# One-bank sums for the feed-forward outputs, one chain of 1/rms for two tiles, and masks made on GpSimd before the diff attention

## Chip, core and metric

The kernel runs on one core of one Trainium2 chip. The metric is the device time of one execution in microseconds (us). The core has a matrix engine (TensorE, PE in the profile), a vector engine (VectorE, DVE), a scalar engine (ScalarE, ACT), a general engine (GpSimd, POOL) and queues that issue transfers (SyncE, SP). Every engine runs its own instructions strictly in the order in which they stand, and waits where an instruction needs a result of another engine.

## What is computed

One sequence of 256 tokens, width 1024, float32. Two layers of a first block come first: each has a feed-forward, a mixer (nsa in layer 0, diff attention in layer 1), and a second feed-forward, all added to `x`. A second block follows (adaLN, moba attention with rope beside an rwkv recurrence) and ends with PEER, which reads far more weights than the rest.

```python
def rmsnorm(x, g):
    xf = x.astype(f32)
    y = xf * lax.rsqrt(jnp.mean(xf * xf, axis=-1, keepdims=True) + EPS)
    return (y * g.astype(f32)).astype(x.dtype)
def swiglu(x, w_in, w_out):
    a, b = jnp.split(x @ w_in, 2, axis=-1)
    return (jax.nn.silu(a) * b) @ w_out
# first_block, layer = 0 (nsa), 1 (diff)
        x = x + 0.5 * swiglu(rmsnorm(x, ffn1_norm[layer]), ffn1_w_in[layer], ffn1_w_out[layer])
        hn = rmsnorm(x, mix_norm[layer])
        x = x + y                         # y = nsa_mixer(hn, ...) or diff_mixer(hn, ...)
        x = x + 0.5 * swiglu(rmsnorm(x, ffn2_norm[layer]), ffn2_w_in[layer], ffn2_w_out[layer])
# diff attention
        p = masked_softmax(sc, dist >= 0)
        a = p[:, :, 0] - lmbda * p[:, :, 1]
        return jnp.einsum('bhts,bhsd->bhtd', a.astype(v.dtype), v)
# ... then o = rmsnorm(o, subln) * (1.0 - lam_init), and o @ w_out
# second_block
    qm = rope_partial(rms_norm(qm.reshape(...), q_norm_g[l]), positions)
    o_rwkv = rwkv7_time_mix(zr, zk, zv, zw, za, zg, ...)
```

## The kernel before

**Stages.** They follow one another: `ffn1_0` (to about 206 us), nsa (391), `ffn2_0` (591), `ffn1_1` (787), `diff` (925), `ffn2_1` (1112), the second block (1400), PEER. `x` lies in SBUF as two tiles of 128 tokens (tile 0 and tile 1).

**Matmuls.** Each is float32 in two parts: a weight tile `raw` is fetched by SP, ACT writes its rounded part `whi` (L124), DVE the rest `wlo` (L125, `raw` minus `whi`), and PE adds three products (L184 to L186) or two (L192, L193). There are four `raw` buffers and six for the split parts. The activations are split alike: PE transposes 128 columns of `x` (`bank<-ident,x`, L234), ACT writes the gained high part `xx` (L270), DVE the low part (L271).

**A feed-forward** keeps the hidden values transposed in `hT` and `lT`. `out_proj` sums the output for tile 0, then for tile 1, each in two halves of 512 columns. A half fills one 2 KiB bank of PSUM; both halves lie in one tile `pair` of two banks. For tile 1 the last weights are taken first for half 0 and then for half 1, so that half 0 is finished earlier; the line `x<-pair,x` (L375, DVE) adds a finished half to `x`. Waits are kept per tile: L375 on half 0 is a reader of the whole pair. The next stage begins with eight transposes of each tile of `x`; those of tile 0 are put ahead by `tc.high_priority(AHEAD_T)`. Beside `ffn2_0`, DVE also adds up `acc` for the second block's adaLN from weights `araw` (L943). The second block takes its transposes of `x` as products with a diagonal `rd` (L958 on DVE, L236 on PE).

**1/rms.** `rstd(i)` squares tile i on ACT (L210) and takes the inverse root of the sum by 14 small instructions (`ms`, `rsg`, `rst`, `rsy`, L214 and L168 to L178). They run on DVE, in the first feed-forward on POOL, one chain for each tile.

**The diff attention** works on four heads and one tile at a time. For each group the probabilities `pr` are subtracted (L861 to L864, DVE) and transposed, L871 multiplies them by `dv` into a bank, ACT squares the result (`dsq`), DVE finds its 1/rms (`dss`, then the same small instructions), and L878 writes the normalised `do`. `do` is transposed (L234), split into `doh` (ACT) and `dol` (DVE, L271), and used by the output matmuls (`bank<-whi,doh`).

**Constants of the second block.** `rope_tables` (sine and cosine of the positions) and `rwkv_consts` stand in the program behind `diff()`; their instructions are drawn into it where an engine's order has room. `rwkv_consts` makes `cmask` and six triangular masks: DVE fills `lm` (L1004), POOL cuts it with three selects (L985), DVE copies two corners of it to `lmask` (L1012). `lm` has two buffers. Nothing reads them before the rwkv stage near 1180 us.

Of the kernel before, what the change touches and what calls it, by code (L numbers as in the profile page):

```python
# [20 lines left out]
F32 = mybir.dt.float32  # L21
# [6 lines left out]
OP = mybir.AluOpType  # L28
# [57 lines left out]
class K:  # L86
# [115 lines left out]

    def rstd(self, i, eps=1e-6, parts=1, early=False):
# [175 lines left out]
    def ffn(self, gain, win, wout, first=False):  # L379
        nc, tc = self.nc, self.tc  # L380
        with ExitStack() as ctx:
# [4 lines left out]
            self.mm = ctx.enter_context(tc.tile_pool(name=self.name("pairs"), bufs=3, space=PSUM, reuse_waits="tile"))  # L386
# [5 lines left out]
            if first:  # L392
# [5 lines left out]
                with tc.manual_schedule(engines={mybir.EngineType.Activation, mybir.EngineType.DVE}):  # L398
# [18 lines left out]
                    rs = [self.rstd(i, early=RSP > 0) for i in range(2)]  # L417
# [27 lines left out]
            for f in range(2, 22):  # L445
# [66 lines left out]
    def head_rs(self, src, n, tag):  # L512
# [22 lines left out]
    def nsa(self):  # L535
        nc, tc, d = self.nc, self.tc, self.d
        with ExitStack() as ctx:
# [46 lines left out]
            for b in range(2):  # L584
                pm = self.proj_chunk("ni", (3 + b,))
                for i in range(2):
# [3 lines left out]
                    r = self.head_rs(kk, 4, "nk")  # L590
# [204 lines left out]
    def diff(self):  # L795
        nc, tc, d = self.nc, self.tc, self.d
        with ExitStack() as ctx:
# [29 lines left out]
            def project(c):  # L827
                pm = self.proj_chunk("di", (c,), by_tile=c == 2)
                for i in range(2):
# [5 lines left out]
                    r = self.head_rs(qk, 8, "dq")  # L835
# [145 lines left out]
    def rwkv_consts(self, pool):  # L981
# [5 lines left out]
        tc_pool = lambda n, b: self.tc.tile_pool(name=self.name(n), bufs=b, reuse_waits="tile")  # L987

        self.cmask = f("cmask", [P, 2, P])
        nc.vector.memset(self.cmask, 1.0)  # L990
        for j in range(2):
            sel(self.cmask[:, j], [[1, P]], j - 1, -1)
        nc.vector.memset(self.cmask[0:64, :, 64:], 0.0)
# [5 lines left out]
        with tc_pool("lm", 2) as tmp:  # L999
            for lv in range(6):  # L1000
                b = 1 << lv
                n = P // (2 * b)
                w = tmp.tile([P, P], F32, name=self.name("lm"), tag="lm")
                nc.vector.memset(w, -1.0)  # L1004
                m = w.rearrange("p (k a u) -> p k a u", a=2, u=b)

                sel(m, [[-2 * b, n], [0, 2], [0, b]], 0, 1)
                sel(m, [[2 * b, n], [0, 2], [0, b]], b - 1, -1)
                sel(m, [[0, n], [1, 2], [0, b]], -1, 0)
                for e in range(2):  # L1010
                    r = slice(64 * e, 64 * e + 64)
                    nc.vector.tensor_copy(self.lmask[r, lv], w[r, r])  # L1012
# [1025 lines left out]
```

## Time and profile before

| | |
|---|---|
| runs | 2220.10, 2226.38, 2228.98 us; median 2226.38 |
| profiled execution | 2228.67 us; span in the trace 2226.9 us |
| busy in the span | PE 98%, DVE 75%, ACT 52%, POOL 1% |
| mean granted clock of PE | 0.987 |

The profiled execution took 2.29 us longer than the median of the runs, and 1.8 us lie around its span. Times in a timeline are counted from the start of the span.

### The profile page before, as it was taken

Reading aid. Unit: us, or ns where it says so; the run is one execution under the profiler, and the core shown is the slowest. Engines: PE = TensorE matmul, PEld = TensorE weight load, DVE = VectorE, ACT = ScalarE, POOL = GpSimd, SP = SyncE. Lnnn points to the kernel's source line nnn. Section 1 sums busy time; section 2 is a strip of 40 time slices with the busy share of each in tenths; the row PEclk is TensorE's granted clock in tenths of the full one; section 3 lists DMA queues with packets and bytes.
Section 4 is the critical chain, followed back from the end, with each engine's and each line's share of the span. In section 5 each row is a group of like instructions: output and inputs, shape, how many; then the busy total and the mean of one; then the engine's idle time right before and its main releaser. Section 6 shows DMA issues by size and latency. Waiting matters only on the chain.

```text
span 2226.9 us, 34952 instructions
## 1 busy us (share of the span) xinstructions
PE 2173.3 (98%) x13218; PEld 1835.4 (82%) x13218; DVE 1677.5 (75%) x3367; ACT 1168.1 (52%) x1853; POOL 33.1 (1%) x75
## 2 busy tenths in 40 slices
PE   8999999999999999899999999999999999999999
PEld 7887646888788876688788777899999998888887
DVE  6866575998688488788487667798858888997555
ACT  6554475654455476455355534445544445555443
POOL 2000000000000000200000000000000000000000
PEclk9999998999999999999999999999999999999999
DMA  6555333877665543355442215545554445545554
GB/s 219 190 190 181 126 106 114 294 273 266 229 218 184 189 153 118 113 189 189 153 146 95 77 48 170 172 159 192 181 180 170 164 169 199 175 175 180 196 191 151
DMA packets 107561, 383.28 MB, mean 172 GB/s; under 512 B 13440, under 2 KB 13824, under 8 KB 107392
## 3 DMA queue, kind: packets, MB, share of 16 engines
q1 hardware_dynamic: 103392, 374.39, 48.7%
q10 hardware_dynamic: 3360, 4.55, 0.7%
q8 instruction: 104, 1.70, 0.3%
q0 software_dynamic: 640, 2.11, 0.3%
q14 instruction: 65, 0.53, 0.1%
HBM read 378.89 MB, written 2.11 MB: 171 GB/s over the span
## 4 chain that ended last, share of the span: by engine, by line
PE 85%; DVE 9%; ACT 2%; DMA 2%; issue 1%; POOL 1%; SPq 0%; ACTq 0%; DVEq 0%; POOLq 0%
PE pair L192 13%; PE pair L193 7%; PE pout L184 5%; PE pout L186 5%; PE pout L185 5%; PE pu L184 5%; PE pu L185 5%; PE pu L186 5%; PE pair L184 4%; PE bank L184 4%; PE pair L186 4%; PE pair L185 4%; PE bank L185 4%; PE bank L186 4%; DVE wlo L125 3%; PE pw L1704 1%
## 5 line engine op out<-in xcount | busy, mean ns | idle before, releaser
L124 ACT ACTIVATE whi<-raw 128x1024 fp32r<-128x1024 f32 x654 | 690.8, 1059 | 704.8 <-PE pout L185 136.5
L125 DVE TENSOR_TENSOR wlo<-raw,whi 128x1024 fp32r<-128x1024 f32 x654 | 797.5, 1222 | 292.6 <-ACT whi L124 283.1
L192 PE MATMUL pair<-xx,whi 128*128 128x512 f32 x1280 | 450.2, 396 | 0.0
L193 PE MATMUL pair<-xx,wlo 128*128 128x256 f32 x1280 | 359.1, 281 | 0.0
L184 PE MATMUL pu<-xx,whi 128*128 128x256 f32 x1024 | 292.6, 286 | 1.1 <-ACT H L1660 1.1
L185 PE MATMUL pu<-xx,wlo 128*128 128x256 f32 x1024 | 289.8, 283 | 0.0
L186 PE MATMUL pu<-xx,whi 128*128 128x256 f32 x1024 | 289.8, 283 | 0.0
L192 PEld LDWEIGHTS pair<-xx,whi 128*128 128x128 f32 x1280 | 240.8, 188 | 56.1 <-issue 0.2
L193 PEld LDWEIGHTS pair<-xx,wlo 128*128 128x128 f32 x1280 | 242.2, 189 | 0.5 <-issue 0.2
L184 PE MATMUL pout<-whi,hs 128*128 128x512 f32 x512 | 201.6, 395 | 1.2 <-ACT hs L1760 1.2
L186 PE MATMUL pout<-wlo,hs 128*128 128x512 f32 x512 | 199.4, 390 | 0.0
L185 PE MATMUL pout<-whi,hs 128*128 128x512 f32 x512 | 199.3, 389 | 0.0
L184 PEld LDWEIGHTS pu<-xx,whi 128*128 128x128 f32 x1024 | 196.4, 192 | 1.3 <-ACT H L1660 1.3
L185 PEld LDWEIGHTS pu<-xx,wlo 128*128 128x128 f32 x1024 | 196.5, 192 | 0.0
L186 PEld LDWEIGHTS pu<-xx,whi 128*128 128x128 f32 x1024 | 196.3, 192 | 0.0
L184 PE MATMUL pair<-whi,hT 128*128 128x512 f32 x352 | 138.9, 395 | 6.6 <-DVE x L375 6.6
L186 PE MATMUL pair<-wlo,hT 128*128 128x512 f32 x352 | 139.5, 396 | 0.0
L185 PE MATMUL pair<-whi,lT 128*128 128x512 f32 x352 | 138.6, 394 | 0.0
L184 PE MATMUL bank<-whi,xx 128*128 128x512 f32 x288 | 118.0, 410 | 0.6 <-DVE rsg L168 0.6
L185 PE MATMUL bank<-whi,xx 128*128 128x512 f32 x288 | 116.0, 403 | 0.0
L186 PE MATMUL bank<-wlo,xx 128*128 128x512 f32 x288 | 115.2, 402 | 0.0
L186 PEld LDWEIGHTS pout<-wlo,hs 128*128 128x128 f32 x512 | 96.1, 188 | 20.5
(564 smaller groups left out, 3509.8 us busy)
## 6 DMA issues: line engine op xcount, KB each, us to landing
raw<-in_pu_dram SPq DMA_DIRECT2D x128, 512.0 KB, 3.5
raw<-in_pv_dram SPq DMA_DIRECT2D x128, 512.0 KB, 3.5
raw<-in_f1i_dram SPq DMA_DIRECT2D x88, 512.0 KB, 3.6
raw<-in_f2i_dram SPq DMA_DIRECT2D x88, 512.0 KB, 4.3
araw<-in_wada_dram SPq DMA_DIRECT2D x48, 512.0 KB, 4.6
raw<-in_f1o_dram SPq DMA_DIRECT2D x44, 512.0 KB, 3.5
raw<-in_f2o_dram SPq DMA_DIRECT2D x44, 512.0 KB, 4.2
raw<-in_wi_dram SPq DMA_DIRECT2D x28, 512.0 KB, 3.4
```

The source lines that it names most:

```text
L124: nc.scalar.activation(hi, raw, AF.Copy)
L125: nc.vector.tensor_tensor(lo, raw, hi.bitcast(F32), op=OP.subtract)
L184: mm(out, lh, rh, start=start, stop=False)
L185: mm(out, ll, rh, start=False, stop=False)
L186: mm(out, lh, rl, start=False, stop=stop)
L192: mm(out, lh, rr, start=start, stop=False)
L193: mm(out[:, 0], ll, rr[:, 0], start=False, stop=stop)
L1704: nc.tensor.matmul(pw[:, t], b[:, t // Q, :, t % Q], a[:, t // Q, :, :, t % Q], start=True, stop=True)
```

## The change

1. `out_proj` of every feed-forward gets single banks: the pool of pairs is closed behind the hidden layer, and six one-bank tiles are opened. With `self.pairs` false, `pair()` hands out two banks with a name each.
2. The first feed-forward calls `rstds`: both squares write one tile of two columns, and one chain of 14 instructions on GpSimd works on both columns.
3. `rope_tables` and `rwkv_consts` are called ahead of `diff()`, and the fills, selects and copies of the masks are all GpSimd's; `lm` has one buffer.
4. Four tags of `head_rs` become one (`hr`), and the slice of its scratch tile is taken earlier. The instructions stay the same.

```diff
+    def rstds(self, early=False):
+        nc = self.nc
+        junk = self.sm.tile([P, D], BF16, name=self.name("junk"), tag="junk", bufs=1)
+        v = self.sm.tile([P, 2], F32, name=self.name("ms"), tag="ms")
+        for i in range(2):
+            nc.scalar.activation(junk, self.x[:, i], AF.Square, accum_out=v[:, i:i + 1])
+        e = nc.gpsimd if early else nc.vector
+        e.tensor_scalar(v, v, 1.0 / D, 1e-6, op0=OP.mult, op1=OP.add)
+        y = self.rsqrt(v, [P, 2], "rs", e=e)
+        return [y[:, i:i + 1] for i in range(2)]
...
-            self.mm = ctx.enter_context(tc.tile_pool(name=self.name("pairs"), bufs=3, space=PSUM, reuse_waits="tile"))
+            inner = ctx.enter_context(ExitStack())
+            self.mm = inner.enter_context(tc.tile_pool(name=self.name("pairs"), bufs=3, space=PSUM, reuse_waits="tile"))
...
-                    rs = [self.rstd(i, early=RSP > 0) for i in range(2)]
+                    rs = self.rstds(early=RSP > 0)
...
+            inner.close()
+            self.pairs = False
+            self.banks(ctx, mm=6)
             self.out_proj(hT, lT, wout, 22, self.add_x(0.5))
             self.extra = None
-            self.pairs = False
...
-        nc.vector.memset(self.cmask, 1.0)
+        nc.gpsimd.memset(self.cmask, 1.0)
...
-        with tc_pool("lm", 2) as tmp:
-            for lv in range(6):
...
-                nc.vector.memset(w, -1.0)
...
-                    nc.vector.tensor_copy(self.lmask[r, lv], w[r, r])
+        for lv in range(6):
+            b = 1 << lv
+            n = P // (2 * b)
+            w = pool.tile([P, P], F32, name=self.name("lm"), tag="lm")
+            nc.gpsimd.memset(w, -1.0)
+            m = w.rearrange("p (k a u) -> p k a u", a=2, u=b)
+            sel(m, [[-2 * b, n], [0, 2], [0, b]], 0, 1)
+            sel(m, [[2 * b, n], [0, 2], [0, b]], b - 1, -1)
+            sel(m, [[0, n], [1, 2], [0, b]], -1, 0)
+            for e in range(2):
+                r = slice(64 * e, 64 * e + 64)
+                nc.gpsimd.tensor_copy(self.lmask[r, lv], w[r, r])
...
+                per = right("per")
+                k.rope_tables(per)
+                k.rwkv_consts(per)
                 if start < 4:
                     k.diff()
             if stop == 4:
                 return finish()
-            per = right("per")
-            k.rope_tables(per)
-            k.rwkv_consts(per)
```

**DVE near the end of the diff attention.** Before, these rows stand ahead of the `do` of the third group of heads (`lm` and `lmask` are the masks, `drs` and `pr` the probabilities of the fourth group, `rst` and `rsy` the 1/rms of the third):

```order
L174 SCALAR_TENSOR_TENSOR rsy_8495<-rst_8496,rsg_8497 128x4
L1004 MEMSET lm_8834 128x128
L171 TENSOR_TENSOR rst_8496<-rsy_8495 128x4
L861 RECIPROCAL drs_8653<-drs_8653 128x2
L1004 MEMSET lm_8841 128x128
...
L171 TENSOR_TENSOR rst_8496<-rsy_8495 128x4
L1012 COPY lmask<-lm_8834 64x64
L864 SCALAR_TENSOR_TENSOR pr_8666<-pr_8666,drs_8653,pr_8659 128x256
...
L1012 COPY lmask<-lm_8841 64x64
L1004 MEMSET lm_8848 128x128
L878 TENSOR_TENSOR do_7426<-bank_8393,rsy_8495 128x512
```

In the changed kernel the same place reads:

```order
L174 SCALAR_TENSOR_TENSOR rsy_8577<-rst_8578,rsg_8579 128x4
L171 TENSOR_TENSOR rst_8578<-rsy_8577 128x4
L877 RECIPROCAL drs_8735<-drs_8735 128x2
L173 SCALAR_TENSOR_TENSOR rst_8578<-rst_8578,dss_8573 128x4
L878 TENSOR_SCALAR drs_8735<-drs_8735,nlam 128x1
L174 SCALAR_TENSOR_TENSOR rsy_8577<-rst_8578,rsy_8577 128x4
L879 TENSOR_SCALAR pr_8741<-pr_8741,drs_8735 128x256
L171 TENSOR_TENSOR rst_8578<-rsy_8577 128x4
L880 SCALAR_TENSOR_TENSOR pr_8748<-pr_8748,drs_8735,pr_8741 128x256
L173 SCALAR_TENSOR_TENSOR rst_8578<-rst_8578,dss_8573 128x4
L174 SCALAR_TENSOR_TENSOR rsy_8577<-rst_8578,rsy_8577 128x4
L894 TENSOR_TENSOR do_7508<-bank_8475,rsy_8577 128x512
```

No row of the masks is left between them.

**PE at the end of `ffn2_0`.** Before, from the last rows of half 0 of tile 1 to the first of the next stage; `pair_5120` holds both halves, `bank_5606` and `bank_5607` take the transposes of tile 1 of `x`:

```order
L185 MATMUL pair_5120<-whi_5406,lT_3758 128x512
L186 MATMUL pair_5120<-wlo_5407,hT_3757 128x512
L184 MATMUL pair_5120<-whi_5400,hT_3757 128x512
L185 MATMUL pair_5120<-whi_5400,lT_3758 128x512
L234 MATMUL bank_5606<-ident,x 128x128 x2
L234 MATMUL bank_5607<-ident,x 128x128 x2
L186 MATMUL pair_5120<-wlo_5401,hT_3757 128x512
...
L186 MATMUL pair_5120<-wlo_5407,hT_3757 128x512
L234 MATMUL bank_5606<-ident,x 128x128
```

In the changed kernel (`bank_5112` is half 0, `bank_5113` half 1):

```order
L185 MATMUL bank_5112<-whi_5399,lT_3745 128x512
L186 MATMUL bank_5112<-wlo_5400,hT_3744 128x512
L184 MATMUL bank_5113<-whi_5393,hT_3744 128x512
L185 MATMUL bank_5113<-whi_5393,lT_3745 128x512
L186 MATMUL bank_5113<-wlo_5394,hT_3744 128x512
...
L186 MATMUL bank_5113<-wlo_5400,hT_3744 128x512
L246 MATMUL bank_5599<-ident,x 128x128 x2
L246 MATMUL bank_5600<-ident,x 128x128 x2
L246 MATMUL bank_5599<-ident,x 128x128
```

The six matmuls of half 1 now write a tile of their own, and all eight transposes of tile 1 stand behind them. The end of `ffn1_0` is changed in the same way.

**DVE at the start of the diff attention.** Before, the low parts of tile 0 of `x` (L271) begin directly behind the first additions to `x`, with `ms` and `rsg` of its 1/rms:

```order
L375 SCALAR_TENSOR_TENSOR x<-pair_6907,x 128x512 x2
L214 TENSOR_SCALAR ms_7364<-ms_7364 128x1
L168 TENSOR_SCALAR rsg_7369<-ms_7364 128x1
L271 SCALAR_TENSOR_TENSOR xx_7336<-bank_7337,cc,xx_7336 128x128
L271 SCALAR_TENSOR_TENSOR xx_7336<-bank_7338,cc,xx_7336 128x128
```

In the changed kernel they begin behind half 0 of tile 1:

```order
L125 TENSOR_TENSOR wlo_7532<-raw_7529,whi_7531 128x1024
L387 SCALAR_TENSOR_TENSOR x<-bank_6906,x 128x512
L283 SCALAR_TENSOR_TENSOR xx_7418<-bank_7419,cc,xx_7418 128x128
L283 SCALAR_TENSOR_TENSOR xx_7418<-bank_7420,cc,xx_7418 128x128
L171 TENSOR_TENSOR rst_7450<-rsy_7449 128x1
L387 SCALAR_TENSOR_TENSOR x<-bank_6907,x 128x512
```

The low parts of tile 0 are later by one addition to `x`, and PE's transposes of tile 0 are later by 14 matmuls.

## Rows read from the trace of the kernel before

**Rows 1.** The page's line of busy time by engine (us, share of the span, instructions), and the chain that ended last, by engine.

```profile
PE 2173.3 (98%) x13218; PEld 1835.4 (82%) x13218; DVE 1677.5 (75%) x3367; ACT 1168.1 (52%) x1853; POOL 33.1 (1%) x75
...
PE 85%; DVE 9%; ACT 2%; DMA 2%; issue 1%; POOL 1%; SPq 0%; ACTq 0%; DVEq 0%; POOLq 0%
```

**Rows 2.** PE's waits over the whole span: what waited, for whom, us in total, times, longest.

```profile
PE bank L871 <- DVE do L878: 7.9, 1, 7.9
PE pair L184 <- DVE x L375: 7.9, 5, 2.5
PE bank L432 <- DVE gu L430: 3.5, 3, 2.4
...
PE bank L234 <- DVE x L375: 2.4, 3, 0.8
```

**Rows 3.** Busy time of the engines in two stretches, the start and the end of the diff attention: stretch and its length, then PE, PEld, DVE, ACT, POOL busy with instruction counts, PE's granted clock, DMA share, GB/s.

```profile
800.00:820.00 20.00, 19.92 (x96) 14.90 (x96) 19.02 (x70) 13.50 (x21) 0.00 (x0) 1.00 0.62 209
...
890.00:905.00 15.00, 6.83 (x32) 5.72 (x31) 8.26 (x33) 1.49 (x5) 12.36 (x18) 0.77 0.11 36
```

**Rows 4.** PE near the end of the diff attention: start, duration, engine, line, operation, count, and in brackets the idle time before and what ended it.

```profile
892.07 0.40 PE L186 MATMUL bank<-wlo,doh 128*128 128x512 f32 x1
...
900.32 1.22 PE L871 MATMUL bank<-dv,pT 128*128 128x128 f32 x4 [7.86 <-DVE do L878]
...
902.19 1.91 PE L871 MATMUL bank<-dv,pT 128*128 128x128 f32 x8
```

**Rows 5.** DVE in the same stretch (same columns), and the sum of its waits for `lm` from 885 to 910 us.

```profile
890.24 0.16 DVE L173 SCALAR_TENSOR_TENSOR rst<-rst,dss 128x4 f32<-128x4 f32 x1
...
891.22 0.66 DVE L173 SCALAR_TENSOR_TENSOR rst<-rst,dss 128x4 f32<-128x4 f32 x1
...
892.00 0.88 DVE L863 TENSOR_SCALAR pr<-pr,drs 128x256 f32<-128x256 f32 x1
...
896.97 0.87 DVE L1012 COPY lmask<-lm 64x64 f32<-64x64 f32 x1 [4.03 <-POOL lm L985]
...
899.58 0.69 DVE L878 TENSOR_TENSOR do<-bank,rsy 128x512 f32<-128x512 f32 x1
...
DVE lmask L1012 <- POOL lm L985: 6.6, 5, 4.0
```

**Rows 6.** POOL in the same stretch, and the selects of `cmask` near 787 us as a group (busy us, mean ns of one, idle before).

```profile
891.08 7.66 POOL L985 TENSOR_SCALAR_AFFINE_SELECT lm<-lm 128x128 f32<-128x128 f32 x6 [103.36 <-DVE rst L171]
899.62 5.69 POOL L985 TENSOR_SCALAR_AFFINE_SELECT lm<-lm 128x128 f32<-128x128 f32 x12 [0.88 <-DVE lm L1004]
...
L985 POOL TENSOR_SCALAR_AFFINE_SELECT cmask<-cmask 128x128 f32<-128x128 f32 x2 | 0.5, 293 | 71.4 <-PE bank L234 71.4
```

**Rows 7.** The end of `ffn2_0`: four rows of PE, two of DVE.

```profile
583.65 0.40 PE L186 MATMUL pair<-wlo,hT 128*128 128x512 f32 x1
...
586.57 0.80 PE L184 MATMUL pair<-whi,hT 128*128 128x512 f32 x1 [2.52 <-DVE x L375]
...
591.02 0.66 PE L234 MATMUL bank<-ident,x 128*128 128x128 f32 x4 [0.78 <-DVE x L375]
...
591.43 0.48 PE L184 MATMUL pair<-whi,xx 128*128 128x512 f32 x1
...
579.80 1.28 DVE L943 SCALAR_TENSOR_TENSOR acc<-araw,silu_c,acc 128x1024 f32<-128x1024 f32 x1 [0.96 <-DMA araw<-in_wada_dram]
...
585.84 0.68 DVE L375 SCALAR_TENSOR_TENSOR x<-pair,x 128x512 f32<-128x512 f32 x1
```

**Rows 8.** PE at the end of `ffn1_0`.

```profile
202.89 0.50 PE L184 MATMUL pair<-whi,hT 128*128 128x512 f32 x1 [1.67 <-DVE x L375]
...
206.19 0.48 PE L184 MATMUL bank<-whi,xx 128*128 128x512 f32 x1
```

**Rows 9.** The ends of `ffn1_1` (three rows of PE) and of `ffn2_1` (two of PE, one of DVE).

```profile
783.74 0.50 PE L184 MATMUL pair<-whi,hT 128*128 128x512 f32 x1 [1.59 <-DVE x L375]
...
786.64 0.66 PE L234 MATMUL bank<-ident,x 128*128 128x128 f32 x4 [0.79 <-DVE x L375]
...
787.05 0.48 PE L184 MATMUL bank<-whi,xx 128*128 128x512 f32 x1
...
1108.83 0.50 PE L184 MATMUL pair<-whi,hT 128*128 128x512 f32 x1 [0.81 <-DVE x L375]
...
1111.89 2.05 PE L236 MATMUL bank<-rd,x 128*128 128x128 f32 x16 [1.40 <-DVE half L1484]
...
1108.68 2.35 DVE L125 TENSOR_TENSOR wlo<-raw,whi 128x1024 fp32r<-128x1024 f32 x2
```

**Rows 10.** The 1/rms of the first feed-forward: POOL (the last row is the end of the second chain), DVE, PE, and PE's stretch behind it (columns as in rows 3).

```profile
19.92 0.19 POOL L176 TENSOR_TENSOR rst<-rst,ms 128x1 f32<-128x1 f32 x1
20.19 1.07 POOL L177 TENSOR_SCALAR rst<-rst 128x1 f32<-128x1 f32 x1
...
31.01 0.19 POOL L178 TENSOR_TENSOR rsy<-rst,rsy 128x1 f32<-128x1 f32 x1
...
23.96 3.49 DVE L125 TENSOR_TENSOR wlo<-raw,whi 128x1024 fp32r<-128x1024 f32 x3
...
32.28 0.44 PE L432 MATMUL bank<-ident,gu 128*128 128x128 f32 x2 [2.44 <-DVE gu L430]
...
34.00:38.00 4.00, 4.00 (x17) 3.41 (x16) 4.00 (x6) 2.85 (x3) 0.00 (x0) 0.62 0.57 177
```

More of the change, by code (lines that the diff above doesn't have):

```diff
@@ L517, in head_rs @@
             m = min(8, n)
-            sq = self.wk.tile([P, 8, 64], F32, name=self.name("sq"), tag="hsq", bufs=1)
-            nc.scalar.activation(sq[:, :m], src[:, b:b + m], AF.Square)
-            nc.vector.reduce_sum(ss[:, b:b + m], sq[:, :m], axis=AX.X)
+            sq = self.wk.tile([P, 8, 64], F32, name=self.name("sq"), tag="hsq", bufs=1)[:, :m]
+            nc.scalar.activation(sq, src[:, b:b + m], AF.Square)
+            nc.vector.reduce_sum(ss[:, b:b + m], sq, axis=AX.X)
         nc.vector.tensor_scalar(ss, ss, 1.0 / 64, 1e-6, op0=OP.mult, op1=OP.add)
@@ L589, in nsa @@
                     nc.scalar.activation(v[:, i, b], pm[i][:, 256:], AF.Copy, scale=rs[i])
-                    r = self.head_rs(kk, 4, "nk")
+                    r = self.head_rs(kk, 4, "hr")
                     kd = self.wk.tile([P, 4, 2, 64], F32, name=self.name("kd"), tag="ckv")
@@ L604, in queries @@
                     nc.scalar.activation(q, pm[i].rearrange("p (h d) -> p h d", h=8), AF.Copy, scale=rs[i])
-                    r = self.head_rs(q, 8, "nq")
+                    r = self.head_rs(q, 8, "hr")
                     nc.vector.tensor_tensor(q, q, r.unsqueeze(2).to_broadcast([P, 8, 64]), op=OP.mult)
@@ L834, in project @@
                     nc.scalar.activation(qk, pm[i].rearrange("p (h d) -> p h d", h=8), AF.Copy, scale=rs[i])
-                    r = self.head_rs(qk, 8, "dq")
+                    r = self.head_rs(qk, 8, "hr")
                     nc.vector.tensor_tensor(qk, qk, r.unsqueeze(2).to_broadcast([P, 8, 64]), op=OP.mult)
@@ L986, in rwkv_consts @@
             m, m, pattern=pattern, compare_op=OP.is_ge, fill=0.0, base=base, channel_multiplier=ch)
[L987 removed]
         self.cmask = f("cmask", [P, 2, P])
[L990 removed]
+        nc.gpsimd.memset(self.cmask, 1.0)
         for j in range(2):
             sel(self.cmask[:, j], [[1, P]], j - 1, -1)
[L993 removed]
+        nc.gpsimd.memset(self.cmask[0:64, :, 64:], 0.0)
         self.eye = f("eye", [P, 64])
@@ L1429, in moba_proj @@
                 nc.scalar.activation(q, pm[i].rearrange("p (h d) -> p h d", h=8), AF.Copy)
-                r = self.head_rs(q, 8, "mo")
+                r = self.head_rs(q, 8, "hr")
                 nc.vector.tensor_tensor(q, q, r.unsqueeze(2).to_broadcast([P, 8, 64]), op=OP.mult)
```

9 lines of the change are left out of this document (removed).

## The prediction, written before the changed kernel ran

> **What bounds the kernel now.** I read the page's busy times first, then the chain that ended last, then PE's waits, and then the timelines around the longest waits. The reader is to see three things. PE is busy for 98% of the span and makes 85% of the last chain, DVE 9% [rows 1]. So a microsecond is gained only where PE stands idle, or where it runs at a lower granted clock; the idle time is 2226.9 less 2173.3, some 54 us in all. Four of PE's waits are touched by the change, and they add up to 7.9 + 7.9 + 3.5 + 2.4 = 21.7 us [rows 2]. That is near the ceiling of the whole change, with what a slow clock behind a wait costs on top. 0.5% of the time is 11 us, about what a measurement of this kernel tells from no change.
>
> **Masks, at the end of diff.** PE ends a matmul near 892.46 and waits 7.86 us for `do` [rows 4]. What is late is on DVE: `do` starts at 899.58, and ahead of it in DVE's order stands a copy of a mask that waits 4.03 us for POOL; the waits for `lm` sum to 6.6 us [rows 5]. POOL is busy for 12.36 of the 15 us [rows 3], in two series of selects from 891.08 on [rows 6]. Beside them DVE's small instructions are longer: the same L173 takes 0.16 us before and 0.66 with the selects, and a `pr` step takes 0.88 [rows 5].
>
> In the new order nothing of the masks stands ahead of `do`. From 890.4 the chain needs some twelve rows: ten small ones of about 0.16, and three `pr` steps of 0.35 to 0.5, that overlap a little. That is about 2.6 us, so `do` starts near 893.0, 6.6 earlier, and PE's wait shrinks from 7.86 to about 1.2. Behind the wait PE runs slow: L871 takes 1.22 for four and 1.91 for eight [rows 4], and the mean granted clock of the stretch is 0.77, between its levels of 1.2 and 2.4 GHz [rows 3]. Its work from 900.32 to 904.1 is 3.8 us; scaled with a clock between half and full, some 1.4 us come back, if the short wait leaves the clock up. The masks between the `dol` steps cost another 0.4. Sum: 6.6 + 1.4 + 0.4 = 8.4 us. Bounds: 6 if the clock falls all the same and a wait of 2 is left, 10 if no wait is left.
>
> **Masks, at the start of diff.** The work doesn't vanish; it goes to about 785 to 820 us, where DVE is busy for 19.02 of 20 us and PE for 19.92 [rows 3]. POOL now does 8 fills, 20 selects and 12 copies. A select alone takes 0.29 [rows 6]; fills and copies on POOL at these sizes I take at the same 0.3, so that without disturbance it is 12 us. In company POOL's operation goes from 0.19 to 1.07 [rows 10], so the series may last 40 us. Nobody waits for it before 1180 us. What counts is what DVE loses: 0.5 for a small instruction that meets a select [rows 5]. DVE also loses work: 13 fills and copies with 6.6 us of waits leave its queue, but at another place. I estimate a delay of 2 to 5 us on DVE in this stretch. PE uses weights that were split some matmuls earlier, and I put what that hides at 5 us, a guess that no row settles; DVE itself has 1 us free here. Cost taken: 0; bounds 0 and 15 (below).
>
> The Trainium skill, GPSIMD Engine Reference, section Key points, says that GpSimd shares its SBUF interfaces with VectorE and contends with DVE instructions that have two SBUF inputs. `wlo` is one. This trace agrees as far as POOL goes (0.19 to 1.07 us), and the rule speaks for the first rival below.
>
> **Single banks, four places.** Half 0 of tile 1 is finished, DVE reads it, and PE's half 1 waits for that reader because both lie in one `pair`: five waits, 7.9 us together [rows 2]. The fifth, 7.9 - 1.67 - 2.52 - 1.59 - 0.81 = 1.3, is at the start of `ffn2_1` and is not touched. Now half 1 is on its own bank, so its six matmuls follow at once, and L375 on half 0 runs beside them.
>
> *End of `ffn1_0`.* Half 0 ends at 202.89 - 1.67 = 201.2 [rows 8]. Six matmuls at 0.23 end near 202.8; DVE's addition (0.69) stands behind a pair of `xx` and is done near 204.1; the transposes take 0.4. The next stage starts near 204.5, not 206.19: 1.7 us.
>
> *End of `ffn2_0`.* Half 0 ends at 584.05, half 1 begins at 586.57 and the next stage at 591.43, with matmuls at 0.80 in place of 0.50 [rows 7, 8]: the clock fell during the wait. DVE's addition starts only at 585.84, since DVE waited 0.96 for an `araw` transfer at 579.80 and then did `acc` for 1.28 [rows 7], and everything behind is late by that; in the new order both stand earlier, and the addition comes as soon as half 0 is done. Half 1 ends near 585.7, both additions near 586.4, the next stage starts near 586.9. Gain 4.5; I take 4.3. If `acc` still stands in the way, 2.5 is left.
>
> *End of `ffn1_1`.* The waits are 1.59 and 0.79 [rows 9]. Half 1 could end near 783.7, and diff start near 784, not 787.05. Against it: the low parts of tile 0 now come behind an addition to `x`, a `posi` transfer is issued among ACT's parts of `xx`, and the cast of it stands ahead of the last pair of `xx` on DVE. I take 1.5; bounds -2 (the cast arrives late, and PE waits for the last two columns of tile 0) and 2.5.
>
> *End of `ffn2_1`.* The wait is 0.81. Behind it two `wlo` (2.35) stand between the two additions, and PE waits 1.40 more [rows 9]. They now come after both additions. Half 1 ends 0.8 earlier and the rest about 0.2 sooner: 1.0, bounds 0 and 2.
>
> **One chain for both tiles.** The second chain on POOL ends at 31.01, and PE's second transposes wait 2.44 until 32.28; then the mean granted clock is 0.62 for 4 us [rows 10], mostly the lower of its two levels (1.2 and 2.4 GHz), which costs 1.5. One chain starts at about 21, when the second square is done. In the new DVE order three `wlo` (before, 3.49 together) come before the first reader, and during them POOL gets an operation done per 1.1 us, afterwards one per 0.27, as from 19.92 to 20.19 [rows 10]. So 3 operations before 21.9, 3 until 25.4, 8 until 27.6. The first transposes then come near 28.4, half a microsecond later than before, the second near 30.7, 1.6 earlier. Net about 1.0, and 0.5 of the clock: 1.5; bounds 0 and 4.
>
> **The rest.** Shared tags of `head_rs` keep every instruction; two loads of ACT's tables go with the new order, on an engine that PE doesn't wait for there. 0, bounds -1 and 1.
>
> **Sum.** 8.4 + 1.7 + 4.3 + 1.5 + 1.0 + 1.5 = 18.4. Against the profiled execution, 2228.67 - 18.4 = 2210.3. That execution lay 2.3 above the median of the runs, so for the median 2226.4 - 18.4 = 2208.0.
>
> **Rivals.**
> 1. *Part of it is given back at the start of diff.* Place: DVE from 785 to 820, POOL's 40 operations beside `wlo`. Price: each that meets a DVE instruction costs DVE 0.5 [rows 5], 20 us if all do; with 5 us hidden, half of them meeting costs PE 5, all 15. Late parts of `xx` can add 2. For: DVE is full there [rows 3]. Against: POOL seems the one that yields, the three `wlo` beside it took 3.49 [rows 10], 1.16 each. Time 2213 to 2223. Chance 0.20.
> 2. *Single banks bring nothing.* DVE's additions and the transposes of tile 1 set the next stage, and PE's wait only moves behind half 1. For: all eight transposes now stand behind half 1, and 2.4 us of PE's waits are for the second addition [rows 2]. Against: the first addition now overlaps six matmuls. Left are masks and 1/rms: 2226.4 - 8.4 - 1.5 = 2216.5. Chance 0.10.
> 3. *Slower.* One mechanism: while POOL holds the port for a select, a `wlo` beside it waits for the whole of it, not 0.5. Place as in 1. Price: a select in company takes 7.66/6 = 1.28 [rows 6]; 40 of them delay DVE by 51 us, of which 5 are hidden, so 2208 + 46 = 2254; it decides from a DVE delay of 23 us on, less than half of that, and beyond 0.5% from 34. Against: the same 1.16 for a `wlo`. Chance 0.05, at 2238 to 2254.
> 4. *The change doesn't do what it says*: the six banks wait for the pairs they are laid over, or POOL starts the masks so late that diff's end still meets them. Then 2222 to 2227. For the banks speaks that their memory was that of pairs; but three pairs rotate, and the two that come first are read long before. Chance 0.05.
>
> **How the numbers follow.** The forecast has 0.60, at 2208, with its own range 2202 to 2214 from the bounds of the terms, which don't fall together. The range is widened upward to rivals 1 and 2: 2199 to 2220. It leaves out rivals 3 and 4, the top of 1, and gains above 27 us. Faster by over 0.5% is below 2215.3: 0.58 of the forecast, 0.10 of rival 1, 0.03 of rival 2, with no more than this from others, 0.72. Slower is rival 3 with a little of other mishaps, 0.05. Within 0.5%: 0.23.
>
> **What would show it.** Right: near the end of diff PE's wait for `do` is at most 2 us, and no `lmask` row is on DVE; POOL has its selects between 785 and 830. PE's waits for `x` between the halves are gone at four ends, and the next stages begin 1.7, 4.3 and about 1.5 us sooner after their feed-forward's half 0. POOL's chain ends near 27.6. Wrong: a `wlo` between 785 and 830 that takes much more than 1.2, or PE idle there by more than 2 us, would be rival 1 or 3; a wait of PE for the second addition that has grown by what the first lost would be rival 2.

## The result, and the profile after

The changed kernel takes 2211.07 us (median of 6, 2204.80 to 2216.43) beside 2220.64 of the kernel before on the same chip: ratio 0.9949, interval [0.9930, 0.9969]. By the ratio that is 11 us (the two medians lie 9.6 apart) of the 18.4 that the sum gave. The profiled execution took 2207.99 us. Two executions took far longer than all others, 4967 us (the profiled one of experiment e9) and 3546 us (one of the kernel before beside it), and are left out of every number.

The page of the changed kernel, its busy times:

```profile
PE 2162.8 (98%) x13218; PEld 1828.9 (83%) x13218; DVE 1676.9 (76%) x3347; ACT 1166.0 (53%) x1851; POOL 38.9 (2%) x81
```

PE's waits over the whole span, as in [rows 2]:

```profile
PE bank L246 <- DVE xx L283: 5.0, 2, 4.2
...
PE bank L184 <- DVE gu L468: 3.0, 3, 1.0
PE pair L184 <- DVE x L387: 2.7, 1, 2.7
PE bank L445 <- DVE gu L443: 2.1, 1, 2.1
```

Against [rows 2]: 7.9 for `do` and the waits for `x` between two halves are gone, and 3.5 for the first 1/rms became 2.1. The 2.7 at the start of `ffn2_0` was there before (2.61, put down to ACT). New are two waits: 5.0 for low parts of `x` (L283) and three of 1.0 for `gu` of the hidden layer.

Stage lengths, each from PE's first matmul of the stage to the next one's first, by the timelines of PE (in = hidden layer, out = output sums and transposes behind them):

| us | ffn1_0 in, out | nsa | ffn2_0 in, out | ffn1_1 in, out | diff | ffn2_1 in, out | rest |
|---|---|---|---|---|---|---|---|
| before | 141.5, 64.7 | 186.9 | 128.0, 70.4 | 129.5, 66.2 | 138.3 | 124.0, 65.2 | 1112.4 |
| after | 138.6, 63.6 | 177.3 | 131.1, 64.3 | 128.5, 63.7 | 137.6 | 125.1, 65.0 | 1111.4 |
| e7 | 136.7, 63.7 | 176.1 | 131.5, 64.3 | 128.5, 65.2 | 132.1 | 124.0, 65.0 | 1111.7 |
| e10 | 137.7, 60.9 | 183.4 | 131.0, 64.3 | 129.5, 62.5 | 137.1 | 124.0, 63.6 | 1112.1 |

The profiled spans differ by 20.6 us. Of these 9.6 lie in nsa, which the change leaves alone; nearly all of them are the granted clock there (last section). The stages don't all hold the same work before and after. Four matmuls on `acc` (L933 before, L949 after; they hold PE for some 1.7 us) have come from the output of `ffn2_0` into its hidden layer:

```profile
549.07 1.88 PE L933 MATMUL bank<-acc,ones 128*128 128x512 f32 x4
```

```profile
509.35 1.88 PE L949 MATMUL bank<-acc,ones 128*128 128x512 f32 x4
```

So the two parts of `ffn2_0` are read together (198.4 before, 195.4 after), and of its hidden layer's 3.1 more the rest is mostly clock, 0.83 in the first 10 us where the kernel before has 1.00. Diff attention, where 8.4 were forecast, shortened by 0.7; but in the changed kernel it holds 16 transposes of `x` that before stood beside it, eight in the output of `ffn1_1` and eight in the hidden layer of `ffn2_1`. From the start of that output to the end of that hidden layer, where both kernels do the same, 328.4 became 326.5: 2.0 us.

**The end of diff attention came out as forecast.** PE and DVE there, to be set beside [rows 4, 5]:

```profile
881.50 0.71 PE L887 MATMUL bank<-dv,pT 128*128 128x128 f32 x4 [1.00 <-DVE do L894]
882.49 1.06 PE L887 MATMUL bank<-dv,pT 128*128 128x128 f32 x8
...
880.75 0.69 DVE L894 TENSOR_TENSOR do<-bank,rsy 128x512 f32<-128x512 f32 x1
```

The wait fell from 7.86 to 1.00 (1.2 forecast), and the matmuls behind it from 1.22 and 1.91 to 0.71 and 1.06. With the transposes between them they took 1.7 us less.

**The start of diff attention gave most of it back.** PE at the start:

```profile
767.19 0.40 PE L184 MATMUL bank<-whi,xx 128*128 128x512 f32 x1
...
769.47 0.39 PE L185 MATMUL bank<-whi,xx 128*128 128x512 f32 x1
774.03 1.97 PE L246 MATMUL bank<-ident,x 128*128 128x128 f32 x8 [4.17 <-DVE xx L283]
...
778.35 0.63 PE L186 MATMUL bank<-wlo,xx 128*128 128x512 f32 x1
778.78 0.47 PE L184 MATMUL bank<-whi,xx 128*128 128x512 f32 x1
```

DVE in the same stretch, and POOL's selects beside it:

```profile
768.00 0.60 DVE L283 SCALAR_TENSOR_TENSOR xx<-bank,cc,xx 128x128 fp32r<-128x128 f32 x2
768.52 1.44 DVE L1010 COPY eye<-ident 64x64 f32<-64x64 f32 x1
769.97 1.59 DVE L1011 COPY eye<-ident 64x64 f32<-64x64 f32 x1
771.58 0.15 DVE L830 TENSOR_SCALAR dgq<-cc 128x1 f32<-128x1 f32 x1
...
771.71 0.60 DVE L283 SCALAR_TENSOR_TENSOR xx<-bank,cc,xx 128x128 fp32r<-128x128 f32 x2
772.23 1.03 DVE L1409 CAST posf<-posi 128x2 f32<-128x2 int32 x1
...
773.63 0.60 DVE L283 SCALAR_TENSOR_TENSOR xx<-bank,cc,xx 128x128 fp32r<-128x128 f32 x2
...
768.11 1.65 POOL L1001 TENSOR_SCALAR_AFFINE_SELECT lm<-lm 128x128 f32<-128x128 f32 x1
...
769.87 3.37 POOL L1001 TENSOR_SCALAR_AFFINE_SELECT lm<-lm 128x128 f32<-128x128 f32 x2
```

Eleven matmuls into the projection PE comes to the eight transposes of tile 1 of `x`. They reuse the two banks that tile 0's transposes filled. The last two pairs of low parts read from them (L283 at 771.71 and 773.63, each pair reads both banks) stand on DVE behind two copies of `eye`, the second also behind the cast of `posi`. PE waits 4.17, the transposes hold it for 1.6 (1.97 until the last is done), and the seven matmuls until 778.78 start 0.43 to 0.57 apart instead of 0.23, 1.5 in all. That is 7.3 us (4.2 + 1.6 + 1.5) of the 8.6 that the end had gained (6.9 of the wait and 1.7).

**The waits of 1.0** are the tenth matmul of an output sum, the first on the fourth bank; and POOL's one chain of 1/rms, its three slow operations and its last, with PE behind it:

```profile
141.85 0.50 PE L184 MATMUL bank<-whi,hT 128*128 128x512 f32 x1 [0.97 <-DVE gu L468]
...
21.30 1.06 POOL L177 TENSOR_SCALAR rst<-rst 128x2 f32<-128x2 f32 x1
...
24.71 0.20 POOL L176 TENSOR_TENSOR rst<-rst,ms 128x2 f32<-128x2 f32 x1
...
26.38 0.20 POOL L178 TENSOR_TENSOR rsy<-rst,rsy 128x2 f32<-128x2 f32 x1
...
27.66 0.44 PE L445 MATMUL bank<-ident,gu 128*128 128x128 f32 x2 [2.13 <-DVE gu L443]
30.41 0.63 PE L445 MATMUL bank<-ident,gu 128*128 128x128 f32 x2
```

### The profile page after: what moved, and what is told of

Read it like the earlier page. It is cut to its first block, busy times and chain, and to the rows that moved or that the text cites. A ratio compares the mean times of both kernels' runs of the same rounds, so it can differ in the third digit from the quotient of the medians.

```text
span 2206.3 us, 34927 instructions
## 1 busy us (share of the span) xinstructions
PE 2162.8 (98%) x13218; PEld 1828.9 (83%) x13218; DVE 1676.9 (76%) x3347; ACT 1166.0 (53%) x1851; POOL 38.9 (2%) x81
## 4 chain that ended last, share of the span: by engine, by line
PE 86%; DVE 9%; ACT 2%; DMA 2%; issue 1%; POOL 0%; SPq 0%; DVEq 0%; ACTq 0%
PE pair L192 13%; PE bank L184 7%; PE bank L185 7%; PE bank L186 7%; PE pair L193 7%; PE pout L184 5%; PE pout L186 5%; PE pout L185 5%; PE pu L184 5%; PE pu L186 5%; PE pu L185 5%; DVE wlo L125 3%; PE pw L1718 1%; ACT whi L124 1%; PE bank L715 1%
## 5 line engine op out<-in xcount | busy, mean ns | idle before, releaser
L184 PE MATMUL bank<-whi,hT 128*128 128x512 f32 x352 | 138.7, 394 | 3.0 <-DVE gu L468 3.0
L185 PE MATMUL bank<-whi,lT 128*128 128x512 f32 x352 | 139.0, 395 | 0.0
L186 PE MATMUL bank<-wlo,hT 128*128 128x512 f32 x352 | 137.9, 392 | 0.0
```

What stands on the lines that cost most here:

```text
L184: mm(out, lh, rh, start=start, stop=False)
L185: mm(out, ll, rh, start=False, stop=False)
L186: mm(out, lh, rl, start=False, stop=stop)
```

## Experiments

All results in one table. "At 0.991" is the mean of a kernel's runs, each moved to the same mean granted clock by 1.8 us for 0.001, the slope that the runs of all kernels together show; its uncertainty is 0.5 to 1.5 us (the kernel before: 2220.9 from 63 runs). The last column runs from the start of the output of `ffn1_1` to the end of the hidden layer of `ffn2_1` (the kernel before: 328.4), so that the same transposes lie in it for every kernel. Diff and the last column are of one profiled execution each, with the granted clock that it had.

| kernel | median us | ratio to before | at 0.991 | diff, us | with its neighbours, us |
|---|---|---|---|---|---|
| changed | 2211.07 | 0.9949 [0.9930, 0.9969] | 2213.2 | 137.6 | 326.5 |
| e1 all but the masks | 2218.24 | 0.9982 [0.9963, 1.0001] | 2215.1 | 140.9 | 330.1 |
| e2 masks alone | 2218.38 | 0.9974 [0.9952, 0.9997] | 2218.7 | 138.1 | 325.0 |
| e3 `eye` on GpSimd | 2213.53 | 0.9951 [0.9935, 0.9967] | 2212.6 | 138.1 | 327.0 |
| e4 constants inside diff | 2213.23 | 0.9944 [0.9923, 0.9964] | 2213.0 | 134.7 | 325.0 |
| e5 sixth bank | 2213.29 | 0.9945 [0.9924, 0.9966] | 2214.1 | 138.2 | 327.0 |
| e6 rope behind diff, `eye` on GpSimd | 2206.04 | 0.9922 [0.9895, 0.9950] | 2210.0 | 131.8 | 320.7 |
| e7 both behind diff | 2207.25 | 0.9926 [0.9900, 0.9953] | 2211.7 | 132.1 | 321.3 |
| e8 one 1/rms chain alone | 2222.94 (one run) | | | 139.1 | 329.2 |
| e9 free banks | 2206.41 | 0.9916 [0.9889, 0.9943] | 2206.4 | | |
| e10 = e7 + e9 | 2204.46 | 0.9903 [0.9878, 0.9929] | 2205.6 | 137.1 | 323.6 |
| e11 = e10, rope in `ffn2_1` | 2203.85 | 0.9897 [0.9868, 0.9925] | 2207.0 | 135.2 | 321.7 |

**e1_no_masks.** The changed kernel without its third part:

```diff
-                per = right("per")      # ahead of k.diff()
-                k.rope_tables(per)
-                k.rwkv_consts(per)
+            per = right("per")          # behind it, masks on VectorE and GpSimd as before
```

> The changed kernel without its third part: rope tables, masks and their place are those of before; single banks, one 1/rms chain and the shared tag stay. Theory A (the masks' part gives back at the start of diff, in PE's wait of 4.17 us and the slow clock behind it, nearly all of the 8 us that it gains at the end): the diff stage lasts about 138 us, as in both kernels; PE waits 7.9 us for do near the end of diff again and under 1 us for xx at its start; time 9 to 11 us under before, ratio 0.995 to 0.996. Theory B (the masks' part brings the 8.4 us of the forecast, and the other parts were oversized): time only 2 to 4 us under before, ratio 0.998 to 0.999.

PE's wait for `do` in this kernel:

```profile
891.02 1.23 PE L887 MATMUL bank<-dv,pT 128*128 128x128 f32 x4 [5.14 <-DVE do L894]
```

With the masks where they were, the wait for `do` is there again, 5.14. The output stages already have their new lengths (64.3 for `ffn2_0`), so these belong to the banks. The time is not that of theory A, though: 0.9982 is theory B's, and diff took 140.9, with a second wait of 1.6 for `do` and the granted clock down to 0.66 near its end. By the ratios the masks' part is worth 0.0033 (the changed kernel beside e1), 7 us; at equal clock it is 2.

**e2_masks_only.** The kernel before with the third part alone, and the shared tags, without which it has no room in SBUF (the hunks of the diff shown above).

> The kernel before with the third part alone (and the shared tags of head_rs, whose smaller scratch makes room for the constants). Theory A: the wait for do falls from 7.9 to about 1 us, a wait of about 4 us for xx at the start of diff appears, the diff stage stays at 137 to 139 us, time 0 to 2 us under before, ratio 0.999 to 1.0. Theory B: time 7 to 9 us under before, ratio 0.996 to 0.997.

PE waits 0.18 for `do`, yet diff takes 138.1 as before: waits of 0.61, 2.52, 1.10 and 1.65 have come near its start, the longest again of tile 1's transposes, behind the two copies of `eye` (1.44 and 1.60 here):

```profile
788.83 0.66 PE L234 MATMUL bank<-ident,x 128*128 128x128 f32 x4 [2.52 <-DVE dgs L816]
```

So the loss there doesn't need the single banks. With its neighbours diff is 3.5 shorter than before. The ratio, 0.9974, lies between the two theories (6 us, 2 at equal clock). The two ratios add up to nearly that of the changed kernel (0.0018 + 0.0026 beside 0.0051).

**e3_eye_pool.**

```diff
-        nc.vector.tensor_copy(self.eye[0:64], self.ident[0:64, 0:64])
-        nc.vector.tensor_copy(self.eye[64:], self.ident[64:, 64:])
+        nc.gpsimd.tensor_copy(self.eye[0:64], self.ident[0:64, 0:64])
+        nc.gpsimd.tensor_copy(self.eye[64:], self.ident[64:, 64:])
```

> The changed kernel with the two copies of eye on GpSimd in place of VectorE, where they took 1.44 and 1.59 us beside the selects against 0.12 and 0.19 before. Theory A1 (the copies, held up by GpSimd's selects, make the parts of xx late): PE's wait for xx at the start of diff falls from 4.2 to about 1.3 us, the clock behind it stays up, time 4 to 5 us under the changed kernel, ratio to before 0.992 to 0.993. Rival A2 (the parts of tile 0 are late because of their place behind the additions to x and three whi, whatever GpSimd does): the wait stays above 3 us, ratio 0.995.

DVE, and PE's wait:

```profile
776.73 0.90 DVE L1409 CAST posf<-posi 128x2 f32<-128x2 int32 x1 [1.18 <-DMA posi<-in_pos_dram]
777.66 1.72 DVE L1412 TENSOR_SCALAR ang<-posf 128x2 f32<-128x2 f32 x3
778.48 0.90 DVE L283 SCALAR_TENSOR_TENSOR xx<-bank,cc,xx 128x128 fp32r<-128x128 f32 x2
...
779.46 1.88 PE L246 MATMUL bank<-ident,x 128*128 128x128 f32 x8 [4.19 <-DVE xx L283]
```

The wait stays (4.19). Without the copies DVE comes to the cast before `posi` has landed, waits 1.18, and the last low parts are as late as before. The copies alone are not the cause; e6 and e7 take away more of what stands ahead of the low parts.

**e4_consts_in_diff.** Both calls behind the transposes of `diff()` in the program:

```diff
+            self.rope_tables(per)       # in diff(), ahead of v = pr.tile(...)
+            self.rwkv_consts(per)
```

> The changed kernel with rope tables and masks called inside diff, behind the transposes and 1/rms of x, so that the parts of tile 0 stand as early as before; GpSimd still makes the masks at the start of diff, and eye is still copied by VectorE, now behind tile 0's parts. A1: the copies still take about 1.5 us each, but delay tile 1 only, whose parts PE needs 5.5 us later: PE's wait at the start of diff is under 1 us, diff lasts about 131 us, time 5 to 7 us under the changed kernel, ratio to before 0.991 to 0.993. A2 expects the same time, with copies of 0.2 us. If the cost only moves to tile 1, a wait of 2 us or more shows 5 to 8 us after diff's first matmul and the ratio is 0.994 to 0.995.

PE's waits near the start:

```profile
785.89 0.50 PE L185 MATMUL bank<-whi,xx 128*128 128x512 f32 x1 [1.50 <-DVE xx L283]
...
793.63 0.50 PE L184 MATMUL bank<-whi,xx 128*128 128x512 f32 x1 [2.88 <-ACT qk L852]
```

The first wait shrinks to 1.50, another of 2.88 follows; the time is that of the changed kernel. The cost has moved, the last of the three cases expected.

**e5_bank5.**

```diff
+        if nf == 22:
+            spare = self.bank(self.mm, 512)
+            pms[1][1] = self.bank(self.mm, 512)
```

> The changed kernel with the fourth sum of out_proj (tile 1, half 1) in the sixth bank in place of the fourth. Theory: the fourth bank was the last pair's, so PE's first matmul into it waits 1.0 us for the addition that reads that pair (gu, L468), in three of the four feed-forwards; in the sixth bank these three waits are gone and nothing else moves: 3 us under the changed kernel, ratio to before 0.993 to 0.994. Rival: the wait is for the hidden values and not for the bank; then it stays at 1.0 in another row and the ratio is 0.995.

The three waits stayed at 0.99 to 1.02. At first this spoke for the rival. It tested nothing: a bank tile that nothing writes gets no place, and in the compiled program the sums lay in banks 2, 7, 6 and 5, as in the changed kernel, with the last pair in 4 and 5. As a second measurement of the changed kernel it gives 0.9945.

**e6_rope_back** and **e7_no_move.** In e6 `rope_tables` goes back behind `diff()` and `eye` is on GpSimd; in e7 both calls go back, and only the engine of the masks is changed:

```diff
-                per = right("per")
-                k.rope_tables(per)
-                k.rwkv_consts(per)
                 if start < 4:
                     k.diff()
...
+            per = right("per")
+            k.rope_tables(per)
+            k.rwkv_consts(per)
```

> The changed kernel with rope_tables behind diff again, as before, the masks still called ahead of it, and eye copied by GpSimd. Theory C (tile 1's transposes use the two banks that tile 0's last low part still reads, and that part stands behind what was called ahead: the copies of eye, and the cast of posi that waits for its transfer and its followers, slowed by GpSimd): with neither in the way, PE's wait of 4.2 us at the start of diff falls under 1 us, diff lasts 131 to 133 us from its first matmul, time 5 to 7 us under the changed kernel, ratio to before 0.991 to 0.993. Theory D (GpSimd's selects beside the low parts are the cause by themselves): GpSimd makes the same masks at the same time, so a wait of 2 to 4 us for xx stays, ratio 0.994 to 0.995.

> The changed kernel with both calls behind diff, as before: only the engine of the masks is changed, not the place of the call. GpSimd has nothing else to do and makes the masks at the start of diff all the same. Theory C: the wait of 4.2 us for xx is gone; the copies of eye on VectorE, about 1.5 us each beside the selects, now stand among tile 1's parts and cost PE 1 to 3 us some 5 to 12 us after diff's first matmul; diff 133 to 135 us, ratio 0.992 to 0.994. Theory D: a wait of 3 to 4 us for tile 0's parts stays, ratio 0.995. That the masks come back to the end of diff (wait for do above 2 us) would mean that the move, and not the engine, took them away.

In e7, all waits of PE near the start of diff (its first row is the transposes of tile 1), and what ACT does ahead of the second `qk`:

```profile
765.49 0.66 PE L246 MATMUL bank<-ident,x 128*128 128x128 f32 x4 [0.16 <-DVE x L387]
...
782.08 0.50 PE L184 MATMUL bank<-whi,xx 128*128 128x512 f32 x1 [3.05 <-ACT qk L850]
...
775.64 1.28 ACT L1424 ACT_TABLE_LOAD   x1
...
777.06 2.94 ACT L124 ACTIVATE whi<-raw 128x1024 fp32r<-128x1024 f32 x3
...
781.36 0.67 ACT L850 ACTIVATE qk<-bank,rsy 128x512 f32<-128x512 f32 x1
```

The transposes are ahead of the projection again, the wait of 4.17 for low parts is gone in both (0.39 and 0.16 are left, for `x`), and diff takes 132. GpSimd made the same masks beside the same low parts, so theory D falls. PE's wait for `do` is 0.99 in e7: the masks don't come back to the end. So the engine alone is enough to take them away from there; whether the move alone would have been, with the fills and copies left on DVE, no run tested. e1 and e7 differ only in the engine of the masks and the buffers of `lm`: 330.1 and 321.3 with the neighbours of diff, 8.8 apart, and ratios of 0.9982 and 0.9926. The move, put on top, cost 5.2 there in these profiles (326.5). In time the correction is worth 0.0023 to 0.0027 of the ratio, 5 to 6 us (1.5 to 3 at equal clock); the intervals overlap with that of the changed kernel. A wait of 2.6 to 3.1 for `qk` is left.

**e8_rstds_only.** The kernel before with `rstds`:

```diff
-                    rs = [self.rstd(i, early=RSP > 0) for i in range(2)]
+                    rs = self.rstds(early=RSP > 0)
```

> The kernel before with the one chain of 1/rms alone. By the forecast the second transposes of gu come 1.6 us sooner and the first 0.5 later: the two waits of 0.73 and 2.44 us become one of 2 to 2.5 or two of 1.3 and 0.8, and the first matmul of out_proj in ffn1_0 comes at 139.5 to 140.5 us, not 141.5. The changed kernel had it at 138.6; if it is there with this part alone, the rest of those 2.9 us belongs to it too (the clock behind the wait), else to the banks or to the start of the program.

PE behind the chain:

```profile
27.73 0.44 PE L444 MATMUL bank<-ident,gu 128*128 128x128 f32 x2 [2.10 <-DVE gu L442]
```

The output of `ffn1_0` starts at 137.64, 3.9 us sooner than before (141.5), and sooner than the 139.5 to 140.5 expected.

**e9_free_banks.** The changed kernel with its sums in banks 2, 3, 6 and 7:

```diff
-            self.banks(ctx, mm=6)
+            self.banks(ctx, mm=2, sa=2, pa=2)
...
+        if nf == 22:
+            for _ in range(2):
+                self.nc.vector.memset(self.bank(self.sa, 512)[:, :1], 0.0)
+            pms[1] = [self.bank(self.pa, 512) for _ in range(2)]
```

> The changed kernel with the sums of the four feed-forwards in the banks 2, 3, 6 and 7 instead of 2, 7, 6 and 5. In the compiled program of the changed kernel the last pair (f = 21) lies in banks 4 and 5, so that the fourth sum, in bank 5, waits for that pair's last reader; the run that was to free it (e5) had changed nothing, because sums that are never written get no bank: its compiled program still had 2, 7, 6 and 5. Here two single-element writes on VectorE hold banks 4 and 5 (0.1 to 0.2 us each, nothing waits for them). Theory B (the bank it lies in makes the wait): the three waits of 0.97, 1.01 and 1.01 us in the outputs of ffn1_0, ffn1_1 and ffn2_1 are under 0.2 us each and the time is about 3 us under that of the changed kernel: ratio to the kernel before about 0.9935, profiled waits for gu L468 gone. Rival R (something else holds the fourth sum): waits of about 1 us stay at the tenth matmul, ratio 0.995 as for the changed kernel.

0.9916, at equal clock 6.8 us under the changed kernel. Its profile is not read; the rows are those of the next kernel.

**e10_no_move_banks**, e7 and e9 together.

> Both corrections together: the tables and masks called behind diff as in the kernel before, and the sums in banks 2, 3, 6 and 7. Theory: the two gains add, diff at 132 us (e7: 132.06), the waits for gu under 0.2 us, ratio 0.9925 - 3/2221 = 0.991, median about 2204 us. Rival: the second cannot be seen beside the spread of the runs (ratio 0.9925 again) though the waits are gone from the profile.

All of PE's longest waits in the span (its line L449 is the first 1/rms):

```profile
PE pair L184 <- DVE x L391: 4.4, 2, 2.6
PE bank L248 <- DVE rd L978: 3.5, 1, 3.5
PE bank L184 <- ACT qk L854: 2.6, 1, 2.6
PE bank L449 <- DVE gu L447: 2.3, 2, 2.1
```

No wait for `gu` at the outputs is left, so the bank it lies in made the wait. Three of the four output stages are shorter than in the changed kernel, by 2.7, 1.2 and 1.3; of the first, 1.4 are the transposes of tile 1, which have gone into the next stage, so that some 3.8 are gained, 3 expected. That the runs show more (6.8 and 6.1 at equal clock, for e9 and for e10 beside e7) is not explained by these rows. The ratio, 0.9903 [0.9878, 0.9929], lies just below the interval of the changed kernel: e10 beats both kernels. Diff took 137.1 and not 132: eight transposes have come into it, and the clock fell there (last section).

**e11_rope_in_ffn.**

```diff
+                if rope and f == 4:
+                    with tc.issue_after(last.ins):
+                        self.rope_tables(rope)
```

> As e10, and the rope tables issued behind the lT of f = 4 of the last feed-forward (ffn2_1), where VectorE and ScalarE have time, instead of where they drift to at the start of diff. Theory C: the 2.6 to 3.1 us wait of the second projection for qk (ScalarE, L850) comes from the sine table load (1.28 us), sin and what waits for the last low parts behind posf and ang; without them it is under 1.5 us, diff 130 to 131 us, ffn2_1's input no longer than 125.5 us, ratio 0.990. Rival D: the wait for qk stays at 2.5 us or more (the weight splits whi ahead of qk are enough for it), diff 132; or the table load holds up a Silu in ffn2_1 and its input is over 126 us.

PE's two waits near the start of diff:

```profile
783.50 0.50 PE L184 MATMUL bank<-whi,xx 128*128 128x512 f32 x1 [1.37 <-ACT qk L857]
...
788.71 0.79 PE L862 MATMUL bank<-ident,qk 128*128 128x128 f32 x4 [1.94 <-DVE qk L859]
```

The wait for `qk` falls to 1.37, but 1.94 for DVE's `qk` follows it: 3.3 together, no less than before. The rope tables made part of the first wait (which of their instructions, the sine's table load or another, this run doesn't separate); taking them away only shows the next. The time is that of e10.

## Why the prediction was right, and which steps failed

**Direction and range held** (2199 to 2220; the forecast's own 2202 to 2214). The sum was 7 us too large. That the time still came within 3 us of 2208 is in part luck: the forecast started from a median of 2226.4, and the kernel before took 2220.64 beside the changed one. 11 us off 2226.4 would have been 2215, outside 2202 to 2214. By the prediction's own sign, PE idle by more than 2 us at the start of diff, what came is rival 1 or 3, and rival 3 falls with `wlo` (below).

**The step that failed: "Cost taken: 0" for the start of diff.** It asked what POOL's work would do to `wlo`, and answered rightly that little: `wlo` kept 1.22 to 1.24 beside the selects, so rival 3 falls. What was lost lay elsewhere, in three things that the prediction had each seen alone: small DVE instructions grow beside a select (`eye`, 0.12 and 0.19 before, 1.44 and 1.59 after; the cast 0.17 and 1.03), the `posi` cast stands ahead of the last low parts, and the transposes of tile 1 come late. The step on `ffn1_1` named the cast and put at most 2 us on it, as a delay of "the last two columns". It did not follow the transpose banks: two of them, whose last readers are those low parts, and behind them eight transposes that stood inside the projection. Rival 1 had place and size (5 us and more), not the mechanism. Small: DVE lost 20 instructions (3367 to 3347), not 13.

**Masks at the end of diff:** 8.4 forecast; the wait gave 6.9 and the faster matmuls 1.7. Right; but of the two things changed, place and engine, the place isn't needed: in e7 the engine alone does it.

**Single banks.** `ffn2_0`: 4.3 forecast; its output fell by 6.0 (70.4 to 64.3 in every kernel with the banks), of which 1.7 are the matmuls on `acc` that moved, so 4.3. Beside e8, where that output took 69.1 without the banks, it is 3.1. `ffn1_0`: 1.7 and 1.1; `ffn2_1`: 1.0 and 0.2; both lost 1.0 to the bank of the last pair, which e10 gave back. The prediction priced that under rival 4, all or nothing, arguing that two of three pairs are read early; the fourth sum was on the third. `ffn1_1`: 1.5 and 2.4, but eight transposes had only gone over into diff; in e1 and e7, where they stay, it is 1.0. Rival 2 falls.

**One 1/rms chain:** 1.5 forecast; the hidden layer of `ffn1_0` shortened by 2.9, in e8 alone by 3.9. The chain is nearly as worked out: three operations at 1.1, then one per 0.27, its last at 26.4 (27.6 forecast) and PE at 27.66 (28.4). PE's waits for `gu` fell from 3.17 to 2.13, the 1.0 forecast. The 0.5 of the clock did not come in this execution: the low stretch, 34 to 38 us before [rows 10], lies behind the new wait at 28 to 32. The rest of the 2.9 lies ahead of the chain, where PE waited 0.7 less for `x` from memory and, from 9 to 13 us, had twice the granted clock for most of the time. First the kernel before, then the changed one:

```profile
9.00:13.00 4.00, 4.00 (x14) 3.17 (x15) 3.11 (x9) 2.56 (x6) 0.00 (x0) 0.59 0.88 355
```

```profile
9.00:13.00 4.00, 4.00 (x23) 3.31 (x22) 3.05 (x8) 2.71 (x8) 0.00 (x0) 1.00 0.86 350
28.00:32.00 4.00, 4.00 (x17) 3.53 (x17) 3.24 (x5) 2.85 (x6) 0.00 (x0) 0.57 0.50 183
```

From 34 to 38 us it is now 1.00. In e8 it is 1.00 in all three stretches. Of the ten profiles with one chain, e5 starts as slowly as the two without it do, and still ends that layer at 138.2; whether the faster start belongs to the change, no run shows.

By stages the 20.6 us between the two profiles are 3.9 in `ffn1_0`, 9.6 in nsa, 2.9 in `ffn2_0`, 1.0 in the hidden layer of `ffn1_1`, 2.0 from there to the end of the hidden layer of `ffn2_1`, and 1.2 behind it. Much of it is clock, in nsa and at the starts of the program and of `ffn2_0`, so no sum of these stages makes the 11 us of the runs.

## What to carry to other kernels

Where work moves to an idle engine at another place, list what then stands ahead of the last reader of every buffer that the matrix engine needs next there, and price a small instruction beside the moved work at its longest, not its mean. First try the engine alone, without the move. Before the lengths of a stage are compared, count its instructions: work can have crossed its border. When a pool is laid over another's memory, look up which new tile lies on the buffer that is read last; an experiment on placement is valid only if the compiled placement differs.

## What the runs showed of the hardware

**A small DVE instruction beside a select often ends with the select.** The first copy of `eye` ends at 769.96, the select beside it at 769.76; the second at 771.56, where the next select, half of 3.37 from 769.87, ends at 771.55. The `posf` cast ends at 773.26, the second select at 773.24. Not every one does: `dgq` at 771.58 took 0.15 beside the same select, and the low parts at 771.71 their 0.60. The Trainium skill, SBUF — State Buffer, section SBUF: two separate sides, says that VectorE and GpSimd share a pair of ports as an exclusive lock: whichever of a GpSimd instruction and a VectorE instruction in a two-port mode, or with two SBUF inputs, starts first has it for its whole length, and the other is blocked. The ends of these copies agree with it. That the selects themselves take 1.65 to 1.69 here and 0.29 alone [rows 6], more than both durations together, it doesn't give, and no run explains it. `wlo`, which reads two tensors, kept 1.22 to 1.24 in its own duration.

**The clock in nsa stays down for longer in some executions than in others.** Stretches of the kernel before, then of the changed one:

```profile
330.00:340.00 10.00, 8.97 (x29) 3.31 (x27) 3.04 (x20) 4.70 (x19) 0.00 (x0) 0.50 0.01 2
340.00:350.00 10.00, 10.00 (x45) 5.04 (x45) 4.24 (x16) 4.77 (x16) 0.00 (x0) 0.50 0.00 1
```

```profile
310.00:320.00 10.00, 9.17 (x49) 4.24 (x50) 3.69 (x22) 4.82 (x14) 0.00 (x0) 0.76 0.01 2
...
330.00:340.00 10.00, 10.00 (x75) 5.35 (x74) 7.90 (x30) 9.27 (x32) 0.00 (x0) 1.00 0.00 1
340.00:350.00 10.00, 9.28 (x45) 4.78 (x45) 6.53 (x29) 6.38 (x21) 0.00 (x0) 1.00 0.32 120
```

From 330 to 350 us PE runs at 1.2 GHz (0.50) in the kernel before and at 2.4 in the changed one, whose clock fell earlier and for less long (0.76 from 310 to 320). PE's longer waits are the same in both (1.39, 0.78, 0.42, 0.51 and 1.02 us). nsa takes 176 to 177 us in the changed kernel, e6 and e7, and 183 to 187 in the other profiles. Diff does it too: e10 has e7's source there, but takes 137.1 and not 132.1. About 0.9 us is eight transposes that have come into it; most of the rest is one stretch:

```profile
869.30:879.30 10.00, 10.00 (x29) 6.74 (x29) 6.21 (x23) 4.82 (x16) 0.00 (x0) 0.52 0.16 52
```

So one profile's stage lengths are read only with the granted clock beside them. At equal clock the change is worth 7.7 us, by the plain ratio 11; whether it also lifts the clock, by the waits it takes away, or was lucky with six runs, stays open, as does what ends such a stretch early in one execution and late in the next.
